# A hybrid decoder trunk on one core: the DeltaNet meta chunk as one padded block for two heads, key norms from a diagonal, loads issued ahead

## The chip, the core and the metric

The kernel runs on one core of one Trainium2 chip. The metric is the device time of one execution, in microseconds (us). The engines are TensorE (PE, with its weight loads as PEld), VectorE (DVE), ScalarE (ACT), GpSimd (POOL) and SyncE (SP, which here issues transfers). Each engine runs its own instructions in order; semaphores order them against each other.

## What is computed

Two layers over 528 tokens (16 learned meta tokens and 512 of the input) with 1024 channels: a forgetting attention with its feed-forward part, then a gated DeltaNet with its feed-forward part. The change touches the DeltaNet alone. Its core, per head of 128 channels (8 heads), with q and k normalised and chunks of up to 64 tokens in the reference:

```python
q = l2norm(q) * Dh ** -0.5;  k = l2norm(k)           # x * rsqrt(sum(x*x) + 1e-6)
dec = exp(where(i >= j, gc_i - gc_j, -inf))          # gc: running sum of the gates in a chunk
A = where(i > j, (k @ k.T) * dec * beta_i, 0)
W, U0 = triangular_solve(I + A, [k * beta * exp(gc), v * beta])
qk = (q @ k.T) * dec
# per chunk, in order:
U = U0 - W @ S.T
O = (q * exp(gc)) @ S.T + qk @ U
S = g_last * S + U.T @ (k * exp(gc_last - gc))
# then rmsnorm(O, o_gain) * silu(og) and the output projection
```

Everything is float32. The dense products split each float32 operand into a high and a low part, and sum three products.

## The kernel before

The tokens stand in two halves, 272 and 256 columns. A weight block of 128 output channels is a *unit*: `load` brings it in by SP, ACT makes its high part (L285), DVE or POOL its low part (L292), and `dense` (L312) runs 24 matmuls of 128x128 weights on 256 or 272 columns per half. L312 is most of TensorE's work everywhere.

The DeltaNet heads (`dn_heads`) run in four groups `g` of two heads (`NG = 2`, index `hl`). Here chunks are `CH`: one of the 16 meta tokens (`ci` 0) and four of 128 tokens. `DNSEQ` orders the units of K, V, Q, output gate (H) and the first half of the output projection (P). Each K, Q or V unit is followed by a causal convolution and a silu on ACT, DVE and POOL (`conv_tile`, L748 to L766, `proj`, L995 to L1004).

The rest of a group is a set of generators that a small planner, `Flow`, weaves in between the dense matmuls. Each `yield t` says when, in estimated TensorE time, the next step is issued; `flow.pe` advances that time, by 0.33 for three dense matmuls. The constants are `T_HOP`, `T_SUMS`, `T_BLOCKS`, `T_STEP`, `T_INV` and `T_OUT`. The steps are:

- `decays`: a transfer `gcr` of the gate sums, broadcast to all partitions, and exp(gc_i - gc_j) into `QD` (L1044, L1047).
- `gram_k`: squares of K on ACT (L1011), sums over the channels as matmuls with a column of ones (L1020), the norms' powers on POOL (L1063), then the products K with K (L1075), scaled into `AT` (L1082). `gram_q` does the same for Q against K (L1020, L1099, L1107), with one more transfer, `eg` (L1109), on the buffers of `gcr`.
- `solve_meta`: the inverse of the meta chunk's 16x16 block as a product of powers; all of its matmuls are 16x16, one per head (L1129, L1137).
- `solve`: the four 128-token chunks. Their 32x32 diagonal blocks go to DRAM (`dA`) and come back with one block on each partition (`AB`); POOL inverts them in 31 steps of two instructions (L1177, L1178); the result goes to DRAM (`dR`) and comes back as `Rc` (L1188). DVE transposes it into `Tc` (L1189), DVE and ACT copy it into the diagonal of `AT` (L1192), and four rounds of small matmuls (L1199 to L1235) finish the inverse.
- `scan`: chunk by chunk, transposes of V and K (L1256, L1257), K with the state S (L1260), `VB` (L1262, L1265), `U` (L1270, L1272), the new S (L1277, L1283) and the output product `po` (L1289, L1291). ACT copies it to `OU` and squares it (L1296, L1297).
- `heads_out`: the output norm's power on POOL (L1309), the scaling of `OU` on POOL (L1312), a transpose back on TensorE (L1316) and the gate.

A head's K, Q or V takes one of 16 buffers (`hd_tile`); when none is free, `flow.until` issues waiting steps, with no dense matmul between, until a scan has given its buffers back. A scan waits for the scan before it. PSUM has eight banks: two for dense results, two for `g` (sums and gram products), two for `s` (scan), one for `o` (`po`), one shared by `t` and `l`.

Dense matmuls and the scan's matmuls keep the order in which they were written (`tok`); the others, and all other engines, are placed by the build's scheduler.

## Time and profile before

| what | us |
|---|---|
| runs, median of 3 | 1601.74 (1598.82 to 1602.18) |
| the profiled execution | 1601.35 |
| its span, first to last instruction | 1599.4 |
| DeltaNet heads, as shown below | about 825 to 1174 of the span |
| TensorE, dense matmuls (L312) in the chain that ended last | 65% of the span |

Times in the profile count from the span's start. A row of a timeline has start, duration, engine, line, operation, out<-in, shapes and count, and in brackets the idle time ahead of it with what ended it. A matmul's duration contains its latency; what a matmul costs in a stream is the distance to the next one's start. A row that groups instructions has count, then busy time and mean ns of one, then the idle time ahead of them.

### The profile page before, as it was taken

To read this page: it belongs to the slowest core of one execution; us is meant where nothing else is said; L and a number is where in the kernel's file an instruction comes from. 1 tells how busy PE (TensorE), PEld (TensorE's weight loads), DVE (VectorE), ACT (ScalarE), POOL (GpSimd) and SP (SyncE) were. 2 spreads that over 40 slices of the span, in tenths; PEclk is the share of its full clock that TensorE was granted. 3 is DMA by queue.
4 is the path that set the end of the run, shared out by engine and by line. 5 is a ranking of instruction groups with operands and counts; after the bars stand their busy time and mean duration, and the time that the engine had idled before them with its cause. 6 is when DMAs were issued, how large, how long until landed. Compare 5 with 4: busy or idle time off the path is not lost.

```text
span 1599.4 us, 33295 instructions
## 1 busy us (share of the span) xinstructions
PE 1525.8 (95%) x12630; PEld 1486.8 (93%) x12630; DVE 1123.4 (70%) x2629; ACT 815.4 (51%) x1925; POOL 495.8 (31%) x993
## 2 busy tenths in 40 slices
PE   8999999999999999999789899899989999999996
PEld 6999999899999999999789798898989999999996
DVE  7888888948974675674978665676569864765764
ACT  6677777735643442343564456545456543432441
POOL 6434443025300010012556475654154200100112
PEclk9999999999999999999799998999999999999998
DMA  5232222422223222222323322222141323323321
GB/s 175 89 89 79 75 78 85 134 65 82 84 83 100 93 85 88 93 93 72 107 75 90 90 61 71 68 77 61 50 150 66 91 82 106 92 82 106 93 67 53
DMA packets 63327, 139.04 MB, mean 87 GB/s; under 512 B 18584, under 2 KB 31288, under 8 KB 62784
## 3 DMA queue, kind: packets, MB, share of 16 engines
q1 hardware_dynamic: 62544, 134.55, 28.1%
q8 instruction: 99, 1.62, 0.4%
q0 software_dynamic: 480, 2.15, 0.4%
q14 instruction: 60, 0.49, 0.1%
q10 hardware_dynamic: 144, 0.22, 0.0%
HBM read 131.54 MB, written 5.36 MB: 86 GB/s over the span
## 4 chain that ended last, share of the span: by engine, by line
PE 74%; DVE 11%; POOL 5%; DMA 4%; ACT 3%; issue 3%; SPq 1%; POOLq 0%; DVEq 0%; ACTq 0%
PE ps L312 65%; POOL PR L1177 2%; POOL RB L1178 2%; DVE h L412 1%; DVE bt L411 1%; DVE wl L292 1%; PE av L698 1%; DMA w<-wflat 1%; DVE cv L764 1%; DMA gcr<-gcd 1%; PE pt L678 1%; DVE xl L378 1%; ACT wh L285 1%; PE s L1277 1%; DVE qr L577 1%
## 5 line engine op out<-in xcount | busy, mean ns | idle before, releaser
L312 PE MATMUL ps<-xh,wh 128*128 128x256 f32 (+4 forms) x2464 | 717.6, 293 | 16.8 <-DVE ub L748 9.2
L312 PE MATMUL ps<-xl,wh 128*128 128x256 f32 (+4 forms) x2464 | 710.8, 289 | 3.4 <-DVE xl L378 3.0
L312 PE MATMUL ps<-xh,wl 128*128 128x256 f32 (+4 forms) x2464 | 713.6, 290 | 0.0
L312 PEld LDWEIGHTS ps<-xh,wh 128*128 128x128 f32 (+1 forms) x2464 | 469.6, 192 | 22.8 <-DVE ub L748 6.3
L312 PEld LDWEIGHTS ps<-xl,wh 128*128 128x128 f32 (+1 forms) x2464 | 471.1, 191 | 7.4 <-DVE xl L378 4.6
L312 PEld LDWEIGHTS ps<-xh,wl 128*128 128x128 f32 (+1 forms) x2464 | 471.1, 191 | 1.0
L285 ACT CAST wh<-w 128x1024 fp32r<-128x1024 f32 (+3 forms) x226 | 225.1, 997 | 189.5 <-PE ps L312 166.7
L292 DVE TENSOR_TENSOR wl<-w,wh 128x1024 fp32r<-128x1024 f32 (+4 forms) x191 | 220.6, 1156 | 99.3 <-ACT wh L285 98.7
L764 DVE SCALAR_TENSOR_TENSOR cv<-ub,prm,cv 128x256 f32<-128x256 f32 (+2 forms) x494 | 243.8, 498 | 38.4 <-ACT cv L755 29.5
L312 PE MATMUL ps<-ah,wl 128*128 128x256 f32 (+2 forms) x704 | 199.5, 284 | 0.0
L312 PE MATMUL ps<-ah,wh 128*128 128x256 f32 (+2 forms) x704 | 199.3, 283 | 0.0
L312 PE MATMUL ps<-al,wh 128*128 128x256 f32 (+2 forms) x704 | 199.1, 283 | 0.0
L755 ACT ACTIVATE cv<-ub,prm 128x256 f32<-128x256 f32 (+2 forms) x224 | 113.8, 511 | 146.3 <-DVE ub L748 146.2
L748 DVE TENSOR_TENSOR ub<-ps,r 128x256 f32<-128x256 f32 (+2 forms) x224 | 95.4, 428 | 101.5 <-PE ps L312 100.6
L353 POOL TENSOR_TENSOR ssq<-ssq,sq 128x256 f32<-128x256 f32 (+2 forms) x98 | 90.5, 926 | 144.5 <-ACT sq L352 143.0
L312 PEld LDWEIGHTS ps<-ah,wh 128*128 128x128 f32 x704 | 132.6, 189 | 0.0
L312 PEld LDWEIGHTS ps<-al,wh 128*128 128x128 f32 x704 | 132.5, 188 | 0.0
L312 PEld LDWEIGHTS ps<-ah,wl 128*128 128x128 f32 x704 | 132.4, 188 | 0.0
L751 POOL COPY cy<-ub 128x2 f32<-128x2 f32 (+1 forms) x112 | 38.0, 341 | 279.3 <-DVE ub L748 277.7
L292 POOL TENSOR_TENSOR wl<-w,wh 128x512 fp32r<-128x512 f32 x70 | 95.0, 1377 | 72.1 <-ACT wh L285 56.8
L747 POOL COPY ub<-cy 128x2 f32<-128x2 f32 (+1 forms) x112 | 31.3, 280 | 197.1 <-DVE cv L764 160.0
L786 ACT ACTIVATE gl<-cv 128x272 f32<-128x272 f32 (+2 forms) x88 | 36.7, 418 | 42.0 <-DVE cv L764 41.7
(308 smaller groups left out, 2454.5 us busy)
## 6 DMA issues: line engine op xcount, KB each, us to landing
w<-wflat SPq DMA_DIRECT2D x176, 512.0 KB, 3.5
w<-wflat SPq DMA_DIRECT2D x32, 448.0 KB, 3.3
cB<-cdram SPq DMA_DIRECT2D x16, 264.0 KB, 3.3
w<-wflat SPq DMA_DIRECT2D x16, 256.0 KB, 2.7
h<-h SPq DMA_DIRECT2D x8, 272.0 KB, 5.3
cB<-cdram SPq DMA_DIRECT2D x16, 136.0 KB, 3.0
h<-h SPq DMA_DIRECT2D x8, 256.0 KB, 5.0
AB<-dA SPq DMA_DIRECT2D x16, 128.0 KB, 3.2
```

What stands on the lines that cost most here:

```text
L285: nc.scalar.copy(wh[:], w32)
L292: eng.tensor_tensor(wl[:, c], w32[:, c], wh[:, c].bitcast(F32), op=ALU.subtract)
L312: tok(nc.tensor.matmul(o, w[:, a], r[:, c0:c1], start=(i == 0), stop=(i == tot - 1)))
L353: nc.gpsimd.tensor_tensor(self.acc[:, :n], self.acc[:, :n], sq[:, :n], op=ALU.add)
L747: nc.gpsimd.tensor_copy(ub[:, 0:c0], carry.pop(ft)[:, :c0])
L748: nc.vector.tensor_tensor(ub[:, c0:c0 + n], ps, r[:, :n], op=ALU.mult)
L751: nc.gpsimd.tensor_copy(c[:, :c0], ub[:, n:n + c0])
L755: nc.scalar.activation(cv, ub[:, c0:c0 + n], AF.Identity, scale=w[c0])
L764: nc.vector.scalar_tensor_tensor(cv, ub[:, i:i + n], w[i], cv, op0=ALU.mult, op1=ALU.add)
L786: nc.scalar.activation(g, cv, AF.Gelu_apprx_tanh)
L1177: nc.gpsimd.tensor_tensor(t, R3[:, 0:a, l:l + 1].to_broadcast([P, a, w]), A3[:, l:l + 1, l + 1:32].to_broadcast([P, a, w]), op=ALU.mult)
L1178: nc.gpsimd.tensor_tensor(R3[:, 0:a, l + 1:32], R3[:, 0:a, l + 1:32], t, op=ALU.subtract)
```

## The change

- **Meta chunk.** The two heads' 16x16 blocks stand at rows and columns 0 and 32 of one 128x128 tile that is otherwise zero. `solve_meta` then runs one full-size matmul for both heads (64 columns moving). The scan's first chunk is its own function, `scan_meta`, with full-size weights, one U product and one output product for both heads.
- **Key norms.** Squares and sums of K go. `gram_k` makes the key products first, and DVE multiplies each with the identity and sums along the rows (a reduce), which gives the norm from the diagonal. The factor 0.25 takes the place of the squares' scale 0.5.
- **Loads.** `decays` issues both `gcr` transfers and yields `T_DMA` before it reads them. `eg` is issued at the start of `gram_q`, on its own two buffers. A second transfer of `dR` writes the diagonal of `AT` in place of the copies (L1192), and the transpose into `Tc` is issued `T_BACK` later.
- **Output.** `po` is squared out of PSUM and scaled out of PSUM by ACT (head 0) and DVE (head 1); the ACT copy and POOL's scaling go. `po` has one bank, and is held until it is scaled.
- **Planner.** Constants change, and dense time is 0.0014 per column and group of three matmuls (0.38 for 272). `KD`, `VB`, `U` go from 3 buffers to 2, `S` from 5 to 4, `OU` from 2 to 1.

The diff, cut to its core:

```diff
-T_BLOCKS = 4
-T_STEP = 0.5
-T_INV = 10
+T_BLOCKS = 8
+T_DMA = 3.5
+T_STEP = 1.0
+T_META = 2.0
+T_BACK = 6
+T_INV = 3
...
-                flow.pe(0.33)
+                flow.pe(0.0014 * (c1 - c0))
...
+        def padded(name, i, w=P):
+            if (name, i) not in zeroed:
+                zeroed[name, i] = dp.tile([P, w], F32, name=f"{name}{i}")
+                nc.vector.memset(zeroed[name, i][:], 0.0)
+            return zeroed[name, i]
...
+                    gcrs.append(dp.tile([P, 272], F32, name="gcr", tag="gc", bufs=2))
+                    nc.sync.dma_start(gcrs[hl][:, :n], gcd[hd:hd + 1, s:s + n].to_broadcast([P, n]))
+                yield T_DMA
...
             def gram_k(half):
-                sqs = squares(half, K)
-                yield T_SUMS
-                pn = psum_tile("g")
-                sums(half, sqs, pn)
...
+                yield T_HOP
+                pgs = gram(half, K)
...
+                        dg = dp.tile([P, P], F32, name="dg", tag="osq")[:, 0:cn]
+                        nc.vector.tensor_tensor_reduce(out=dg, in0=pgs[hl][:, i * 128:i * 128 + cn], in1=ident[:, 0:cn], scale=1.0, scalar=0.0, op0=ALU.mult, op1=ALU.add, accum_out=y[:, c, hl:hl + 1])
+                nc.vector.tensor_scalar(y[:, cs, :], y[:, cs, :], 0.25, EPS, op0=ALU.mult, op1=ALU.add)
...
+            def gram(half, X):
...
+                        nc.tensor.matmul(pgs[hl][:, i * 128:i * 128 + cn], K[hl][:, c0:c0 + 128], X[hl][:, c0:c0 + cn], start=True, stop=True)
...
                 def products(*pairs):
                     ps = psum_tile("l")
-                        for hl in range(NG):
-                            nc.tensor.matmul(ps[:16, (i * NG + hl) * 16:(i * NG + hl) * 16 + 16], a[:, hl, :], b[:, hl, :], start=True, stop=True)
+                    for i, (x, y) in enumerate(pairs):
+                        nc.tensor.matmul(ps[:, i * 64:i * 64 + 64], x[:], y[:, b], start=True, stop=True)
...
+                    nc.sync.dma_start(AT[32 * b:32 * b + 32, :, 32 * b:32 * b + 32], dR[NC * b:NC * b + NC].rearrange("c j r i -> (j r) c i"))
+                yield T_BACK
                 nc.vector.transpose(Tc[:].rearrange("p c i -> p (c i)"), Rc[:].rearrange("p c i -> p (c i)"))
-                for b in range(4):
-                    bs = slice(32 * b, 32 * b + 32)
-                    (nc.scalar.copy if b % 2 else nc.vector.tensor_copy)(AT[bs, :, bs], Rc[bs])
...
+            def scan_meta(MO):
...
+                tok(nc.tensor.matmul(px[0][:, 128:256], st["Rm"][:], VB[:], start=True, stop=True))
...
+                for hl in range(NG):
+                    tok(nc.tensor.matmul(px[hl][:, 0:128], KD[hl][:], U[:], start=True, stop=True))
...
+                tok(nc.tensor.matmul(po[:, 0:128], st["QDm"][:], U[:], start=True, stop=True))
...
-                        nc.scalar.copy(OU[:cn, hl, :], oo)
-                        nc.scalar.activation(sq[:cn, 0:128], OU[:cn, hl, :], AF.Square, scale=128 ** -0.5, accum_out=MO[:cn, ci, hl:hl + 1])
+                        nc.scalar.activation(sq[:], po[:, hl * 128:hl * 128 + 128], AF.Square, scale=128 ** -0.5, accum_out=MO[:, ci, hl:hl + 1])
...
-                    nc.gpsimd.tensor_scalar(ot, ot, mo[:, hl:hl + 1], None, op0=ALU.mult)
+                    (nc.vector.tensor_scalar(OU[:, hl, :], po[:, hl * 128:hl * 128 + 128], mo[:, hl:hl + 1], None, op0=ALU.mult) if hl else
+                     nc.scalar.activation(OU[:, hl, :], po[:, hl * 128:hl * 128 + 128], AF.Copy, scale=mo[:, hl:hl + 1]))
...
-                yield lambda: ("gates", half) in done and (g < 2 or ("scan", g - 2) in done)
+                yield lambda: ("gates", half) in done and (g < 2 or ("scan", g - 2) in done) and (half or not g or ("meta", g - 1) in done)
```

Three places show how the instructions move. The rows give line, operation, out<-in and size; the changed kernel has its own line numbers (dense matmuls are L315, the scan's transposes L1295 and L1296, K with S L1298, U L1305, the new S L1311, the output products L1318 and L1319, the output transposes L1378).

First, TensorE in group 0's scan, just ahead of the next K unit; before, the last chunk's first products:

```order
L312 MATMUL ps<-xh_10425,wh 128x272
L312 MATMUL ps<-xl_10426,wh 128x272
L312 MATMUL ps<-xh_10425,wl 128x272
L1256 MATMUL s<-ident,hd 128x128
L1257 MATMUL s<-ident,hd 128x128
L1260 MATMUL s<-S,hd 128x128
L1256 MATMUL s<-ident,hd 128x128
L1257 MATMUL s<-ident,hd 128x128
L1260 MATMUL s<-S,hd 128x128
L312 MATMUL ps<-xh_10425,wh 128x272
```

The same place of the changed kernel, one chunk earlier:

```order
L1378 MATMUL t<-ident,OU 128x128 x2
L1305 MATMUL s<-VB,ATQD_11241 128x128 x2
L1311 MATMUL s<-U,KD 128x128 x2
L1318 MATMUL o<-S,hd 128x128
L1319 MATMUL o<-U,ATQD_11241 128x128
L1318 MATMUL o<-S,hd 128x128
L1319 MATMUL o<-U,ATQD_11241 128x128
L1295 MATMUL s<-ident,hd 128x128
L1296 MATMUL s<-ident,hd 128x128
L1298 MATMUL s<-S,hd 128x128
```

Before, dense matmuls stand between the steps of every chunk. Now the scan of group 0 is issued later, the buffers of K, Q and V run out first, and the work of its last three chunks stands in one piece of 36 rows with no dense matmul in it.

Second, DVE at the return of group 0's solve; before:

```order
L748 TENSOR_TENSOR ub<-ps,r 128x256
L764 SCALAR_TENSOR_TENSOR cv<-ub,prm,cv 128x272
L1192 COPY ATQD_11250<-Rc 32x8x32 x2
L1064 TENSOR_TENSOR rho<-y,rk 128x4
L764 SCALAR_TENSOR_TENSOR cv<-ub,prm,cv 128x272
L292 TENSOR_TENSOR wl<-w_12379,wh 128x1024
L1189 STREAM_TRANSPOSE Tc<-Rc 128x256
L1065 TENSOR_SCALAR rk<-rk 128x4
L1148 TENSOR_TENSOR Wm<-l,Wm 16x32
```

And in the changed kernel:

```order
L1178 TENSOR_TENSOR Y_11462<-l,ident 64x64
L1104 SCALAR_TENSOR_TENSOR ATQD_11736<-g,ab,ATQD_11736 128x128
L767 SCALAR_TENSOR_TENSOR cv<-ub,prm,cv 128x272
L751 TENSOR_TENSOR ub<-ps,r 128x256
L767 SCALAR_TENSOR_TENSOR cv<-ub,prm,cv 128x272
L295 TENSOR_TENSOR wl<-w_12584,wh 128x1024
L1132 TENSOR_SCALAR eq<-g 128x6
L1228 STREAM_TRANSPOSE Tc<-Rc 128x256
L1180 TENSOR_TENSOR Y_11460<-l,Y_11462 64x64
```

The copies are gone, and the first reader of `Rc` is the transpose, which now stands behind the key step of group 1 (L1104) that it stood ahead of before.

Third, ACT where a chunk's output is made, in a scan of group 0 before:

```order
L1296 COPY OU<-o 128x128 x2
L1138 COPY Wm<-l 16x32
L1262 ACTIVATE VB<-s,rho 128x128
L1297 ACTIVATE osq,MO<-OU 128x128
L1262 ACTIVATE VB<-s,rho 128x128
L1297 ACTIVATE osq,MO<-OU 128x128
L1266 ACTIVATE KD<-s,kd 128x128 x2
```

And in the scan of group 1 after:

```order
L1302 ACTIVATE KD<-s,kd 128x128
L1358 ACTIVATE osq,MO<-o 128x128
L1302 ACTIVATE KD<-s,kd 128x128
L1272 ACTIVATE ATQD_11736<-l 64x8x64
L1374 ACTIVATE OU<-o,MO 128x128
L1307 ACTIVATE U<-s,ub 128x128 x2
L1394 ACTIVATE o_12924<-t,osc 128x128
```

The square reads `po` itself, and the scaling (L1374), which reads POOL's power, stands ahead of the scan's next `U`.

More of the change, by code (lines that the diff above doesn't have):

```diff
@@ L1088, in gram_q @@
                 sqs = squares(half, Q)
+                egs = []
+                for hl in range(NG):
+                    hd = g * NG + hl
+                    egs.append(dp.tile([P, 272], F32, name="eg", tag="eg", bufs=2))
+                    nc.sync.dma_start(egs[hl][:, :n], gcd[hd:hd + 1, s:s + n].to_broadcast([P, n]))
                 yield T_SUMS
@@ new lines, in products @@
+                    return [ps[b, i * 64:i * 64 + 64] for i in range(len(pairs))]
+                nc.vector.tensor_tensor(N[b, b], N[b, b], smask[:], op=ALU.mult)
+                yield T_META
+                ps = psum_tile("l")
+                nc.tensor.transpose(ps[:, 0:P], N[:], ident[:])
+                nc.scalar.copy(NT[b, b], ps[b, b])
+                yield T_META
+                x, y = products((NT, N), (N, NT))
+                nc.scalar.copy(N2T[b, b], y)
+                nc.vector.tensor_copy(N2[b, b], x)
@@ new lines, in scan @@
+                    yield T_HOP + 0.6
+                    if ci < 4:
+                        for hl in range(NG):
+                            tok(nc.tensor.matmul(px[hl][:, 0:128], KD[hl][:], U[hl][:], start=True, stop=True))
+                            flow.pe(0.22)
+                            S[hl] = dp.tile([P, P], F32, name="S", tag="S", bufs=4)
+                            nc.vector.scalar_tensor_tensor(S[hl][:], S0[hl][:], GL[:, g * NG + hl, ci:ci + 1], px[hl][:, 0:128], op0=ALU.mult, op1=ALU.add)
```

219 lines of the change are left out of this document (116 added, 103 removed).

## The prediction

> **What bounds the kernel now.** First the page: busy shares, granted clock by slices, the chain that ended last.
>
> ```profile
> PE 1525.8 (95%) x12630; PEld 1486.8 (93%) x12630; DVE 1123.4 (70%) x2629; ACT 815.4 (51%) x1925; POOL 495.8 (31%) x993
> ...
> PEclk9999999999999999999799998999999999999998
> ...
> PE 74%; DVE 11%; POOL 5%; DMA 4%; ACT 3%; issue 3%; SPq 1%; POOLq 0%; DVEq 0%; ACTq 0%
> ```
>
> TensorE is busy for 95% of the span and holds 74% of the chain: what takes work from it shortens the run, and so does what ends a pause of it. The clock dips in the 20th and the 25th slice (40 us each); the latter, 960 to 1000 us, lies in the DeltaNet heads. Next the table of windows: the heads (825 to 1174 us) and four stretches in which the granted clock was half. Columns: start and end, length, busy time and count of PE, PEld, DVE, ACT, POOL, clock, DMA share, GB/s.
>
> ```profile
> 825.00:1174.00 349.00, 329.30 (x2952) 310.99 (x2950) 229.17 (x640) 181.93 (x529) 177.00 (x427) 0.95 0.28 75
> ...
> 900.70:907.50 6.80, 4.70 (x23) 4.37 (x23) 6.42 (x21) 3.09 (x6) 2.38 (x4) 0.50 0.31 84
> ...
> 975.80:986.00 10.20, 10.20 (x51) 8.31 (x51) 2.09 (x8) 2.69 (x10) 3.37 (x11) 0.50 0.39 100
> 1027.00:1030.40 3.40, 3.15 (x15) 3.07 (x16) 2.62 (x9) 3.04 (x10) 0.00 (x0) 0.50 0.22 45
> 1088.40:1091.90 3.50, 3.50 (x19) 3.50 (x19) 1.58 (x4) 1.82 (x3) 1.92 (x9) 0.51 0.00 0
> ```
>
> In the heads PE pauses for 349.00 - 329.30 = 19.7 us. Three of the half-clock stretches begin in or right behind a pause; the one at 975.8 follows none. The timelines name the pauses (in brackets the idle time before the row, and what ended it):
>
> ```profile
> 899.58 0.70 DVE L1192 COPY ATQD<-Rc 32x256 f32<-32x256 f32 x2 [7.98 <-DMA Rc<-dR]
> ...
> 902.80 0.28 PE L1129 MATMUL l<-Wm 16*16 16x16 f32 x4 [6.14 <-DVE Wm L1148]
> ...
> 957.67 0.41 ACT L1192 COPY ATQD<-Rc 32x256 f32<-32x256 f32 x1 [4.87 <-DMA Rc<-dR]
> ...
> 958.92 0.49 PE L1277 MATMUL s<-U,KD 128*128 128x128 f32 x2 [1.78 <-ACT U L1272]
> ...
> 1020.61 0.33 PE L1316 MATMUL t<-ident,OU 128*128 128x128 f32 x1 [1.96 <-POOL OU L1312]
> ...
> 1025.59 0.35 DVE L1044 SCALAR_TENSOR_TENSOR ATQD<-gcr,COL,dmask 128x128 f32<-128x128 f32 x1 [6.56 <-DMA gcr<-gcd]
> ...
> 1027.25 0.23 PE L1075 MATMUL g<-hd 128*16 128x16 f32 x2 [2.75 <-DVE ATQD L1107]
> ...
> 1088.16 0.33 PE L1316 MATMUL t<-ident,OU 128*128 128x128 f32 x1 [3.27 <-POOL OU L1312]
> ```
>
> In each an engine that runs its instructions in order stands at a late transfer, or POOL is late, with something for PE queued behind. At about 891.6 us DVE reached the Rc copy and waited 7.98 us for its transfer; L1148, for which PE waited, stood six rows behind (the order rows above).
>
> **What leaves PE.** The key sums (half of L1020). Their price is the group's row and one run of eight in PE's timeline:
>
> ```profile
> L1020 PE MATMUL g<-one,sq 128*128 128x1 f32 x160 | 20.0, 238 | 0.7 <-DVE ATm L1082 0.7
> ...
> 856.33 1.05 PE L1020 MATMUL g<-one,sq 128*128 128x1 f32 x8
> 857.24 0.37 PE L312 MATMUL ps<-xh,wh 128*128 128x272 f32 x1
> ```
>
> Eight rows take 857.24 - 856.33 = 0.91 us, 0.114 each. A float32 product is two rows, so the 40 of 80 sums that go are 80 rows: **9.1 us**.
>
> The small products of the meta chunk are priced as stops in the dense stream: from the dense row ahead to the second dense row behind, less two steady steps of 0.12.
>
> ```profile
> 860.70 0.28 PE L312 MATMUL ps<-xh,wh 128*128 128x256 f32 x1
> 860.91 0.26 PE L1129 MATMUL l<-Wm 16*16 16x16 f32 x4
> ...
> 861.33 0.28 PE L312 MATMUL ps<-xh,wl 128*128 128x256 f32 x1
> ...
> 875.01 0.29 PE L312 MATMUL ps<-xh,wl 128*128 128x272 f32 x1
> 875.14 0.38 PE L1099 MATMUL g<-hd 128*128 128x128 f32 x2
> ...
> 875.49 0.28 PE L312 MATMUL ps<-xl,wh 128*128 128x272 f32 x1
> ...
> 881.08 0.28 PE L312 MATMUL ps<-xh,wh 128*128 128x256 f32 x1
> 881.29 0.36 PE L1129 MATMUL l<-Wm 16*16 16x16 f32 x8
> ...
> 881.80 0.28 PE L312 MATMUL ps<-xh,wl 128*128 128x256 f32 x1
> ...
> 914.42 0.28 PE L312 MATMUL ps<-xh,wl 128*128 128x256 f32 x1
> 914.63 0.61 PE L1270 MATMUL s<-VB,Rm 16*16 16x128 f32 x4
> ...
> 915.39 0.28 PE L312 MATMUL ps<-xl,wh 128*128 128x256 f32 x1
> ...
> 918.35 0.28 PE L312 MATMUL ps<-xh,wl 128*128 128x260 f32 x1
> 918.55 0.71 PE L1277 MATMUL s<-U,KD 16*128 16x128 f32 x4
> ...
> 919.95 0.28 PE L312 MATMUL ps<-xl,wh 128*128 128x260 f32 x1
> ```
>
> A step of one product for two heads (four rows of 16x16) costs 0.63 - 0.24 = 0.39, a step of two products 0.72 - 0.24 = 0.48, and a full 128x128 product 0.48 - 0.25 = 0.23. A group has four steps of the first kind and two of the second: 2.52 before. Now a single block serves both heads: 4 x 0.23 + 2 x 0.46 = 1.84 at most, 0.7 less. In the scan the four Rm rows cost 0.97 - 0.24 = 0.73 and the KD and QDm rows 1.60 - 0.24 = 1.36; now there are four full products, 0.92, so 1.2 less. Over four groups: 4 x (0.7 + 1.2) = **7.6 us**. The meta key and query products (full weights for 16 columns) and one output transpose less I leave at nothing.
>
> Here the Trainium skill speaks against the padding: "TensorE: Matmul & The Clock Gate", section "LDWEIGHTS (loading the stationary operand)", has a weight load cost its columns over 1.2 ns, whatever the rows. By that a load of 16 columns is 13 ns and one of 128 is 107; an estimate from it, for the 54 small loads of a group that become 33 full ones, is 0.7 against 3.5 us, 11 us dearer over four groups, and a sum of 1604. The stops above hold their loads and come out the other way; a mechanism like the rule's is a rival below.
>
> **What ends waits.** The diff takes the Rc copies from DVE and ACT (a transfer writes AT, the transpose is issued 6 us later), the OU products from POOL, and starts gcr and eg transfers earlier on buffers of their own. So the pauses of 6.14, 1.78, 1.96, 2.75 and 3.27 us lose their causes: **15.9 us**. With three of them the half-clock stretches behind should go: PE was busy for 4.70 + 3.15 + 3.50 = 11.35 us there, half of which is **5.7 us**. In all 9.1 + 7.6 + 15.9 + 5.7 = **38.3 us**.
>
> **What is added.** (1) In the new order the last three chunks of the first scan stand on PE with no dense row between (above). Each round waits for an ACT and a DVE result, and its transposes (OT) for the output chain:
>
> ```profile
> L1272 ACT ACTIVATE U<-s,ub 128x128 f32<-128x128 f32 (+1 forms) x30 | 9.8, 360 | 5.4 <-PE s L1270 5.2
> L1265 DVE SCALAR_TENSOR_TENSOR VB<-s,COL,VB 128x128 f32<-128x128 f32 x24 | 8.0, 341 | 6.5 <-ACT VB L1262 6.4
> ...
> L1309 POOL TENSOR_TENSOR MO<-MO,mhalf x20: 692/721/1717, 924.4 to 1168.8; 128x2 f32<-128x2 f32 x16, 16x2 f32<-16x2 f32 x4
> ```
>
> At least 3 x (0.36 + 0.34) = 2.1 us. At most also two out-chain waits as long as the longest above, 3.27, and half clock throughout: 26 products at 0.23 = 6.0 us once more; 14.6. I take **9** (2.1, two waits of 1.96, half of the 6.0). (2) At the end two transposes stand right behind the last product that they depend on: 0 if the order is kept by slack, 3.27 at most; **3**. (3) The reduces, 40 on DVE, replace the key sums' squares on ACT:
>
> ```profile
> L650 DVE CUSTOM_DVE_ANT_0 S<-sc,cB 128x264 f32<-128x264 f32 x32 | 13.6, 427 | 0.3
> ...
> L650 DVE DVE_READ_ACCUMULATOR2_ANT st<- 128x1 f32 x96 | 7.9, 82 | 0.0
> ```
>
> No row has 128 columns; the nearest, 264, bounds them: 40 x (0.427 + 0.082) = 20 us of DVE. With DVE at 229 of 349 us the price on the path is 0 to 20; I take a quarter, **5**. (4) ACT and DVE now scale the output out of PSUM and wait for POOL's power (0.72 us, in POOL's queue among the steps of the solve), with conv and weight casts queued behind; PE waits for both. It happens in 20 rounds; a round can cost nothing, or the 1.96 of the nearest row: 0 to 39. I take what the old chain cost, 1.96 + 3.27 = **5.2**. (5) SP issues 16 more transfers of dR, with weight loads queued behind; one issue reads:
>
> ```profile
> 956.12 0.45 SPq L1188 DMA_DIRECT2D Rc<-dR  x1
> ```
>
> That is 16 x 0.45 = 7.2 us of SP in four places, hidden as long as the weights of the next units are loaded ahead; I take 0, and 7.2 if that cover is gone.
>
> Sum against the profiled execution, 1601.35 us (0.4 below the median, 1601.74): 1601.35 - 38.3 + 9 + 3 + 5 + 5.2 = 1585.3. I predict **1585**.
>
> **Rivals.**
> - *Waits only move.* PE's own 16.7 us go, but other waits of the length of the old ones come, and the crowded places cost 12: 1601.35 - 16.7 + 12 = 1596.7. For it: pauses come from one late transfer or another, and all of the order changes. Against: the causes named are taken away. 0.22.
> - *Nothing in the end.* As before, and the reduces also cost their 5: 1601.7, no change. For it: DVE carried 6.42 of the 6.80 us from 900.7. 0.09.
> - *The clock recovers.* The stretch at 975.8 goes too (half of 10.2, 5.1 us), and (1), (3), (4) come out at their low ends, 2.1 + 3: 1601.35 - 38.3 - 5.1 + 5.1 = 1563. 0.12.
> - *Slower: the output chain stalls ACT.* ACT's scale stands right ahead of the scan's next U rows (order above); if POOL's power is late by its queue each round, 20 rounds cost PE 1.96 each, 39 us: 1601.35 - 38.3 + 17 + 39 = 1619. It decides from (38.3 - 17) / 20 = 1.1 us a round. For it: L1309's longest took 1.72 us, and POOL is full during the solve. Against: ACT worked 182 of 349 us. 0.13.
> - *The padding costs.* A stop of four rows took 0.39 and one of eight 0.48: 0.30 fixed and 0.022 a small row, against 0.115 a full row. If the fixed part stays with full products among dense rows, a group pays 24 x 0.115 for 44 x 0.022, 1.8 us more, 7 over four: 1585.3 + 7.6 + 7 = 1600, no change. Against: the full product's stop above, 0.23 in all. 0.04. The skill's rule on weight loads points this way.
>
> The skill's clock rule is weighed too: "TensorE: Matmul & The Clock Gate", section "Part 1: The HAM clock gate (the \"warmup\" mystery)", has the clock halve after an idle window of about 3.4 us. The stretches behind the 6.14 and 3.27 us pauses agree; the one at 975.8, with PE busy throughout, does not. By the rule the crowded scan of (1) would keep full clock and the sum be 3 us lower.
>
> **How the numbers follow.** Forecast 0.40, the rivals 0.22, 0.09, 0.12, 0.13, 0.04. About 0.2%, 3.2 us, is what a measurement can tell from no change. Faster: 0.40 + 0.22 + 0.12 = 0.74; same 0.09 + 0.04 = 0.13; slower 0.13. The range holds forecast, moved waits, no change and padding (0.75) and the upper half of the clock case: 1566 to 1603, and (1) to (3) together at their low ends give 1570, (3) at its high end 1600.
>
> **What would show it.** Right: L1042 (sums) with 80 rows and some 10 us; no 6 us pause of PE behind a DVE wait on Rc; PE's pauses in the heads under 15 us. Wrong: PE waiting for OU from ACT or DVE in many rounds; ACT idle on POOL's power; a half-clock stretch over the first scan's end longer than 7 us; DVE busy above 290 us in the heads.

## The result, and the profile after

The changed kernel takes **1615.97 us** (median of 4 runs, 1615.81 to 1618.67), the kernel before 1600.75 on the same chip: ratio 1.0100, 95% interval 1.0082 to 1.0117. It is slower by 15 us; the prediction had it 16 us faster. The profiled execution has a span of 1614.3 us against 1599.4. The page of the changed kernel (busy time, granted clock in 40 us slices, the chain that ended last):

```profile
PE 1521.4 (94%) x12462; PEld 1489.7 (92%) x12462; DVE 1140.3 (71%) x2765; ACT 801.9 (50%) x1868; POOL 458.2 (28%) x951
...
PEclk9999999999999999999799789999998999999998
...
PE 68%; DVE 11%; POOL 6%; DMA 5%; ACT 4%; issue 3%; SPq 2%; POOLq 0%; DVEq 0%; ACTq 0%
```

PE's share of the chain fell from 74% to 68%: more of the chain is the work of other engines and of transfers. To see what PE lost, the heads are cut in both kernels at the same work: from the first column transpose to dense product 1632 of this phase. The tables of windows (start and end, length, busy time and count of PE, PEld, DVE, ACT, POOL, clock, DMA share, GB/s), before:

```profile
825.42:1181.88 356.46, 336.76 (x3014) 318.45 (x3013) 232.83 (x648) 185.56 (x537) 180.24 (x432) 0.95 0.29 78
```

and after:

```profile
828.40:1194.13 365.73, 328.99 (x2846) 318.83 (x2845) 247.11 (x769) 174.31 (x484) 145.76 (x388) 0.93 0.30 77
```

PE is busy 7.8 us less, and yet the stretch is 9.3 us longer. Its pauses rose from 356.46 - 336.76 = 19.7 to 36.7 us. The half-clock stretches inside, summed from the clock's records, rose from 34.1 to 51.2 us, with PE busy for 31.8 and 46.6 of them; half of that is lost. So **work at full clock fell by 15.2 us** (320.9 to 305.7), **pauses grew by 17.0** and **half clock cost 7.4 more**: +9.2. Another 3.0 us come ahead of the heads (they begin at 828.40, not 825.42) and 2.7 behind: 14.9 in all. What PE waited for in the heads (the table of waits: total us, times, longest), before:

```profile
PE l L1129 <- DVE Wm L1148: 6.1, 1, 6.1
PE t L1316 <- POOL OU L1312: 5.5, 3, 3.3
```

and after:

```profile
PE t L1378 <- ACT OU L1374: 9.9, 4, 4.5
PE ps L315 <- DVE ub L751: 8.8, 4, 3.5
PE s L1305 <- ACT KD L1302: 5.2, 4, 2.6
```

The longest pause of before (6.14, behind a DVE that stood at Rc) is gone; in its place stand many of up to 4.5 us, behind the output's scale, the conv's input and the scan's rows. The wait of the output transposes, behind which two of the pauses in the prediction lie, did not go: it rose from 5.5 us behind POOL to 9.9 behind ACT, which now does the scaling. One cause stands in the views of the tile Rc, which tell who waited for its transfer. Before:

```profile
  ACT ATQD L1192: 14.0, 3
  DVE ATQD L1192: 13.1, 3
```

After:

```profile
  ACT TM L1245: 15.4, 4
  DVE Tc L1228: 12.1, 4
```

27.1 us before, 27.5 after: the same standing, now at the transpose and at the copy behind it, with other rows queued behind that copy. The longest wait of the output transposes, 4.5 us, has this cause, on ACT:

```profile
1042.87 0.40 ACT L1245 COPY TM<-Tc 32x256 f32<-32x256 f32 x1 [6.58 <-DVE Tc L1228]
1043.30 0.37 ACT L1374 ACTIVATE OU<-o,MO 128x128 f32<-128x128 f32 x1
```

The other three (1.7, 1.5 and 2.2 us) come right behind a wait of ACT for POOL's power; the first of them, on ACT and on PE:

```profile
959.12 0.37 ACT L1374 ACTIVATE OU<-o,MO 128x128 f32<-128x128 f32 x1 [2.03 <-POOL MO L1371]
```

```profile
959.54 0.71 PE L1378 MATMUL t<-ident,OU 128*128 128x128 f32 x2 [1.72 <-ACT OU L1374]
```

Progress against dense products shows three places where much is lost. Windows of 24 dense products each (576 to 600, 1056 to 1080, 1536 to 1560), before:

```profile
955.97:968.11 12.14, 9.66 (x138) 8.23 (x137) 8.87 (x25) 9.01 (x26) 2.54 (x5) 1.00 0.27 65
1078.46:1082.72 4.26, 4.26 (x37) 4.09 (x35) 3.64 (x9) 3.19 (x10) 3.85 (x10) 1.00 0.28 65
1170.19:1173.29 3.10, 3.10 (x28) 3.10 (x27) 1.57 (x4) 1.02 (x4) 0.70 (x5) 1.00 0.62 259
```

After:

```profile
955.14:976.25 21.11, 15.23 (x92) 13.24 (x91) 13.29 (x39) 12.16 (x41) 3.55 (x11) 0.84 0.27 55
1076.28:1090.37 14.09, 11.04 (x83) 10.29 (x83) 5.91 (x18) 5.91 (x15) 11.15 (x35) 0.75 0.13 29
1176.50:1185.27 8.77, 6.51 (x43) 5.92 (x41) 3.51 (x10) 3.47 (x11) 1.43 (x5) 0.83 0.35 121
```

The first is the crowded scan of step (1), the third the tail of step (2), the second another piece of solve and scan rows without dense products that no step had. They are 9.0, 9.8 and 5.7 us longer, and the clock falls in each; the rest of the heads is some 15 us shorter. Not all of this is loss, since rows other than dense products also stand in other windows now: pauses make 3.4, 3.0 and 2.3 us of it and half clock 2.6, 2.7 and 1.4; the rest is work that stood elsewhere before.

### The profile page after: what moved, and what is told of

It is laid out like the page before. It is cut to its first block, busy times and chain, and to the rows that moved or that the text cites. A ratio compares the mean times of both kernels' runs of the same rounds, so it can differ in the third digit from the quotient of the medians.

```text
span 1614.3 us, 32996 instructions
## 1 busy us (share of the span) xinstructions
PE 1521.4 (94%) x12462; PEld 1489.7 (92%) x12462; DVE 1140.3 (71%) x2765; ACT 801.9 (50%) x1868; POOL 458.2 (28%) x951
## 4 chain that ended last, share of the span: by engine, by line
PE 68%; DVE 11%; POOL 6%; DMA 5%; ACT 4%; issue 3%; SPq 2%; POOLq 0%; DVEq 0%; ACTq 0%
PE ps L315 62%; POOL RB L1215 3%; POOL PR L1214 3%; DVE h L415 1%; DVE bt L414 1%; DVE wl L295 1%; DMA w<-wflat 1%; PE av L701 1%; DVE cv L767 1%; DVE xl L381 1%; DMA AB<-dA 1%; PE pt L681 1%; DMA gcr<-gcd 1%; ACT wh L288 1%; DVE qr L580 1%
## 5 line engine op out<-in xcount | busy, mean ns | idle before, releaser
L315 PE MATMUL ps<-xh,wh 128*128 128x256 f32 (+4 forms) x2464 | 720.6, 294 | 26.6 <-DVE ub L751 19.1
L315 PE MATMUL ps<-xl,wh 128*128 128x256 f32 (+4 forms) x2464 | 713.4, 290 | 6.1 <-DVE xl L381 6.0
L315 PE MATMUL ps<-xh,wl 128*128 128x256 f32 (+4 forms) x2464 | 716.3, 291 | 0.0
L315 PEld LDWEIGHTS ps<-xh,wh 128*128 128x128 f32 (+1 forms) x2464 | 473.9, 193 | 31.2 <-DVE ub L751 11.9
L315 PEld LDWEIGHTS ps<-xl,wh 128*128 128x128 f32 (+1 forms) x2464 | 474.3, 193 | 10.2 <-DVE xl L381 8.1
L315 PEld LDWEIGHTS ps<-xh,wl 128*128 128x128 f32 (+1 forms) x2464 | 474.1, 193 | 0.9 <-DVE wl L295 0.3
L315 PE MATMUL ps<-ah,wl 128*128 128x256 f32 (+2 forms) x704 | 199.8, 284 | 0.0
L315 PE MATMUL ps<-ah,wh 128*128 128x256 f32 (+2 forms) x704 | 199.6, 284 | 0.0
L315 PE MATMUL ps<-al,wh 128*128 128x256 f32 (+2 forms) x704 | 199.4, 284 | 0.0
L315 PEld LDWEIGHTS ps<-ah,wh 128*128 128x128 f32 x704 | 132.9, 189 | 0.0
L315 PEld LDWEIGHTS ps<-al,wh 128*128 128x128 f32 x704 | 132.7, 189 | 0.0
L315 PEld LDWEIGHTS ps<-ah,wl 128*128 128x128 f32 x704 | 132.6, 189 | 0.0
L814 DVE TENSOR_TENSOR m<-m,ps 128x256 f32<-128x256 f32 (+2 forms) x64 | 27.2, 425 | 42.6 <-PE ps L315 42.5
```

The source lines that it names most:

```text
L315: tok(nc.tensor.matmul(o, w[:, a], r[:, c0:c1], start=(i == 0), stop=(i == tot - 1)))
L814: nc.vector.tensor_tensor(mm, mm, ps, op=ALU.add)
```

## The experiments

In this table every row is one kernel: ratio to the kernel before on the same chip (with interval), and from its trace, cut as above, length of the heads, pauses of PE, half-clock time and PE's work at full clock, in us. The trace is one execution, and executions of one kernel differ: the kernel before took 1596.0 to 1609.3 us in the 29 runs beside p_norm. The last column is rough as well, because it takes half of the busy time at half clock as lost: j_up (316.4) and n_both (318.2) have all rows that PE has before (320.9). Differences of under 5 us in it say little where the half-clock time differs.

| kernel | ratio | length | pauses | half clock | work |
|---|---|---|---|---|---|
| before | 1 | 356.5 | 19.7 | 34.1 | 320.9 |
| changed | 1.0100 (1.0082-1.0117) | 365.7 | 36.7 | 51.2 | 305.7 |
| p_norm | 1.0032 (1.0017-1.0048) | 360.7 | 30.0 | 51.2 | 309.9 |
| p_pad | 1.0017 (1.0002-1.0031) | 353.4 | 26.8 | 37.6 | 311.2 |
| p_out | 1.0010 (0.9995-1.0025) | 357.3 | 19.2 | 37.6 | 322.5 |
| p_plan | 1.0051 (1.0031-1.0071) | 362.1 | 24.7 | 34.1 | 321.2 |
| p_load | 1.0022 (1.0006-1.0037) | 359.4 | 19.7 | 37.6 | 321.3 |
| j_up | 1.0039 (1.0022-1.0056) | 364.9 | 20.4 | 61.4 | 316.4 |
| n_none | 0.9985 (0.9973-0.9997) | 352.2 | 25.9 | 30.7 | 313.7 |
| n_both | 0.9999 (0.9988-1.0010) | 358.7 | 14.1 | 54.6 | 318.2 |
| n_half | 0.9985 (0.9972-0.9998) | 354.3 | 18.7 | 34.1 | 319.7 |
| a_plan0 | 1.0130 (1.0110-1.0150) | 376.7 | 44.6 | 61.4 | 304.6 |
| a_load0 | 1.0073 (1.0055-1.0091) | 364.5 | 36.5 | 54.6 | 302.8 |
| a_back | 1.0127 (1.0106-1.0149) | 373.0 | 42.5 | 51.2 | 307.3 |
| a_jit | 1.0080 (1.0061-1.0098) | 364.6 | 38.3 | 41.0 | 307.0 |
| a_norm0 | 1.0041 (1.0028-1.0053) | 363.9 | 30.3 | 37.6 | 316.5 |
| a_free | 1.0080 (1.0063-1.0097) | 365.3 | 36.8 | 51.2 | 305.2 |
| p_free | 0.9990 (0.9977-1.0004) | 354.1 | 25.3 | 34.1 | 312.6 |
| b_two | 1.0040 (1.0026-1.0055) | 361.6 | 39.7 | 41.0 | 304.1 |
| b_three | 1.0052 (1.0034-1.0070) | 362.5 | 37.7 | 47.8 | 304.6 |

**One part at a time, on the kernel before.** Diagonal norms alone:

```diff
-                sqs = squares(half, K)
-                sums(half, sqs, pn)
...
+                        nc.tensor.matmul(pgs[hl][:, i * 128:i * 128 + cn], K[hl][:, c0:c0 + 128], K[hl][:, c0:c0 + cn], start=True, stop=True)
...
+                        nc.vector.tensor_tensor_reduce(out=dg, in0=pgs[hl][:, i * 128:i * 128 + cn], in1=ident[:, 0:cn], scale=1.0, scalar=0.0, op0=ALU.mult, op1=ALU.add, accum_out=y[:, c, hl:hl + 1])
```

> The kernel before with one part of the change: key norms from the diagonal of the key products (40 reduces on DVE, no key sums on PE, no key squares on ACT), the key products with 128 weight columns for the meta chunk too. All else as before (1600.75 us). Theory A (the 15 us come from scan and solve rows that the planner's constants and the loads push into one piece): the sums' 9.1 us leave PE and nothing crowds: 1590 to 1597. Theory B (the output path costs): the same. Theory C (DVE carries the heads, so the reduces give the gain back): 1599 to 1606, with PE waits behind DVE in the heads up by 5 us or more. Theory D (any change of the order moves waits by several us whatever it is): 1592 to 1612 without a pattern.

1.0032, and 1607 us, just above the range of theory C and inside that of theory D; the 9.1 us do not come. PE's work falls by 11.0 us, pauses grow by 10.3, half clock by 17.1. Much of that is one half-clock stretch of 27.3 us, from 907.24 to 934.54. The padded meta chunk alone (solve_meta and scan_meta of the change):

> The kernel before with one part of the change: the meta chunk of two heads as one zero-padded block in solve and scan, with the steps' due times and smaller buffer counts that came with it. Output path, loads, norms and the other planner constants as before. My prediction put this part at -7.6 us. Theory A: 1592 to 1599. Padding rival (the fixed part of a product stays): 1602 to 1610, and the 33 full products of a group take more of PE than the 54 small ones. Theory D: anything from 1590 to 1612, the difference then being in pauses of PE and not in PE's busy time.

1.0017. The time lies in the range of the padding rival, but its mechanism does not: work falls by 9.7, and the heads are 3.1 us shorter. That is given back ahead of the heads (they begin at 828.45) and behind. The output path alone:

```diff
-                    nc.gpsimd.tensor_scalar(ot, ot, mo[:, hl:hl + 1], None, op0=ALU.mult)
+                    nc.scalar.activation(OU[:cn, hl, :], po[:cn, hl * 128:hl * 128 + 128], AF.Copy, scale=mo[:, hl:hl + 1])
```

(DVE takes the second head.)

> The kernel before with one part of the change: ACT squares the output straight from PSUM and ACT and DVE scale it out of PSUM behind POOL's power; POOL's scaling and ACT's copy are gone. All else as before. Theory B (this chain stalls ACT and with it the scan): 1607 to 1620, with ACT idle on POOL's MO in many rounds and PE's U wait longer than the 5.2 us that it has before. Theory A: 1596 to 1602, the pauses of 1.96 and 3.27 us behind POOL's OU shorter. Theory D: 1590 to 1612.

1.0010, no difference to be told from none; 1604 us lies between theory A and theory B. ACT does stand 11.9 us for POOL's power over 20 rounds, 0.6 a round, and PE's pauses do not grow:

```profile
L1311 ACT ACTIVATE OU<-o,MO 128x128 f32<-128x128 f32 (+1 forms) x20 | 7.2, 359 | 12.0 <-POOL MO L1307 11.9
```

The planner's constants alone:

```diff
-T_BLOCKS = 4
-T_STEP = 0.5
+T_BLOCKS = 8
+T_STEP = 1.0
-                flow.pe(0.33)
+                flow.pe(0.0014 * (c1 - c0))
```

> The kernel before with the planner's constants of the change alone: blocks 8 in place of 4, steps 1.0 in place of 0.5, a dense product booked by its columns. No instruction is added or removed, only moved. Theory A in its plainest form: 1606 to 1615, with the first scan's last chunks in one piece without dense rows and 24 dense rows there taking 20 us in place of 12. Theory B and the padding rival: 1599 to 1603. If it is the loads and not the constants that delay the scan, this one is same, and the loads alone are slower.

1.0051, the dearest part alone, and in the range of theory A. Its first crowded place takes 19.8 us, as expected, and its last 24 dense products 8.57 us in place of 3.10, as in the changed kernel. PE's timeline there:

```profile
1169.96 0.38 PE L1291 MATMUL o<-U,ATQD 128*128 128x128 f32 x2
1173.37 1.06 PE L1316 MATMUL t<-ident,OU 128*128 128x128 f32 x2 [3.03 <-POOL OU L1312]
```

and the window of those 24 products:

```profile
1167.82:1176.39 8.57, 5.43 (x34) 4.95 (x33) 2.51 (x6) 2.87 (x10) 2.65 (x7) 0.78 0.35 122
```

The output transposes stand right behind the last product they depend on: a pause of 3 us, then half clock on the dense products. So the constants alone are enough to make the tail's loss. The loads alone (transfers ahead, AT from a second transfer, transpose 6 us later, T_INV 3 in place of 10):

> The kernel before with the loads of the change alone: gcr and eg transfers issued ahead on their own buffers, the solve's result read into AT by a second transfer, the transpose of Rc planned 6 us after its transfer. My steps put most of the 15.9 us of pauses here. If those pauses go and stay gone: 1585 to 1594. Theory E (they come back elsewhere, as in the changed kernel, where DVE and ACT together stand 27.5 us for Rc, against 27.1 before): 1600 to 1612.

1.0022, as theory E had it: nothing of the 15.9 us comes. The 6.14 us pause is gone and the output transposes wait 2.8 us in place of 5.5, yet PE's pauses are 19.7 us in all, as before. Other waits fill the place, the largest of them short or absent before:

```profile
PE s L1280 <- ACT KD L1276: 6.5, 4, 3.8
PE g L1022 <- ACT sq L1013: 2.5, 1, 2.5
```

**What an order, or a load, costs by itself.** One number moved by 3%:

```diff
-                flow.pe(0.33)
+                flow.pe(0.34)
```

> The kernel before with one number of the planner moved a little: a dense product booked at 0.34 us in place of 0.33. The same instructions, in another order from the heads' solve on. It measures how far an order alone moves the time. Theory D (any other order moves waits by several us): off by 3 to 10 us from 1601, either way. If it stays within 2 us, the +2 to +8 us of the single parts are theirs and not the order's.

1.0039: the same instructions in another order cost 6 us, more than any single part but the constants. A single part's time therefore proves little; only what its trace shows at a place does, or several kernels together. The key norms left out:

> The kernel before with the key norms left out: no key squares, no key sums, a constant in their place; nothing added. PE has 80 rows, about 9 us, less to do and ACT 40 squares less. If the heads are bound by PE's work, 1591 to 1594, and then the reduces of the change are what gave the gain back. Theory E: 1598 to 1604, PE's pauses in the heads up from 19.7 to 25 us or more with nothing added to DVE.

0.9985, as theory E had it: 7.2 us less work, 6.2 us more pauses, 2 us gained. And the reduces added, read by nobody:

> The kernel before with the 40 reduces on DVE added and read by nobody; key squares and sums stay. This is the price of the reduces alone. If DVE's load is what counts (my term of 5, at most 20): 1606 to 1620. If DVE has room there: 1600 to 1604, and the loss with the diagonal norms comes from their place in the chain (power and scales wait for the products), not from DVE's time.

0.9999: 40 reduces on DVE cost nothing that can be told from an order's effect.

**The changed kernel in other orders.** With the constants of before:

> The changed kernel with the planner's constants of before (blocks 4, steps 0.5, a dense product booked at 0.33 us); padding, norms, output path and loads stay changed. The changed kernel takes 1615.97 us; the constants alone cost the kernel before some 8 us (0.5%). Theory A (the constants push scan and solve into places without dense products): 1604 to 1609, the 21 us place at dense product 576 to 600 and the 14 us place at 1056 to 1080 gone or under 2 us longer than before. Theory E (PE's saved work turns into pauses in whatever order, since results of other engines and transfers are awaited): 1610 to 1617, pauses in the heads still over 30 us.

1.0130, above both ranges. The crowded places nearly go, as theory A asked: dense products 576 to 600 take 14.3 us in place of 21.1 (12.1 before), with 0.7 us of pauses and 6.8 us at half clock, and 1056 to 1080 take 3.9. The tail's pause of 2.3 us stays, without half clock. The first place and the tail:

```profile
972.21:986.54 14.33, 13.66 (x144) 13.14 (x143) 6.29 (x19) 7.39 (x24) 1.30 (x4) 0.76 0.11 38
1190.68:1196.83 6.15, 3.84 (x30) 3.46 (x29) 2.00 (x6) 2.67 (x9) 1.43 (x5) 1.00 0.38 127
```

Yet the kernel gains nothing: PE's pauses in the heads are 44.6 us, more than the 36.7 of the changed kernel, and lie elsewhere. With the loads of before (T_INV too):

> The changed kernel with the loads of before: Rc copied to AT by DVE and ACT, transposed at once, gcr and eg read where they were. If the loads are what costs the 15 us: 1598 to 1604. Theory E: 1610 to 1624, like the other orders of the changed kernel (1616 and 1626).

1.0073, in the range of theory E: the loads are not what costs most, and their share is no larger than what an order makes. With T_BACK 12 in place of 6:

> The changed kernel with the transpose of Rc planned 12 us after its transfer in place of 6. In the changed kernel DVE stands 12.1 us for Rc and ACT 15.4 us behind it, in four solves. If the planned distance is what was too short: those waits under 8 us together and 1606 to 1612. If it only delays the solve and what waits for it: 1614 to 1625.

1.0127, as was expected if it only delays: the waits for Rc fell only to 8.4 (DVE) and 13.1 (ACT). With a dense product booked 3% longer:

> The changed kernel with a dense product booked 3% longer (0.00144 us a column in place of 0.0014): the same instructions in another order. With before, j_up (1608) and the changed kernel's other order (1626) it shows whether the orders of the changed kernel lie above those of before. If the change itself costs: 1610 to 1626. If 1616 was a bad draw among orders: 1596 to 1608.

1.0080. Four orders of the changed kernel lie at 1.0080 to 1.0130, above every order of the kernel before that was run (1, 1.0039, 1.0051). That speaks for a cost of the change itself, and against 1616 as a bad draw among orders.

**The norms and their tiles.** The key step of group 0 in the changed kernel (key products on PE, power and first solve step on POOL):

```profile
836.72 0.85 PE L1114 MATMUL g<-hd 128*128 128x16 f32 x6
...
858.52 1.06 PE L1114 MATMUL g<-hd 128*128 128x128 f32 x8
```

```profile
850.99 2.63 POOL L1093 TENSOR_TENSOR rk<-y,mhalf 128x6 f32<-128x6 f32 x1 [3.46 <-DVE y L1092]
...
875.73 0.47 POOL L1214 TENSOR_TENSOR PR<-RB,AB 128x31 f32<-128x31 f32 x1 [1.11 <-DMA AB<-dA]
```

and in the kernel before:

```profile
838.07 1.51 POOL L1063 TENSOR_TENSOR rk<-y,mhalf 128x6 f32<-128x6 f32 x1 [3.44 <-DVE y L1062]
840.37 1.01 POOL L1063 TENSOR_TENSOR rk<-y,mhalf 128x4 f32<-128x4 f32 x1
...
857.96 0.24 POOL L1177 TENSOR_TENSOR PR<-RB,AB 128x31 f32<-128x31 f32 x1 [4.97 <-DMA AB<-dA]
```

Before, the power comes ahead of the products, and both halves' powers stand side by side. Now the products are written first and hold both PSUM tiles of kind "g" until the power is back and the scaling has read them; the second half's products follow 21.8 us behind the first (before, 4.5), and the solve begins at 875.73, not 857.96. To test that, the norms of before in the changed kernel:

> The changed kernel with the key norms of before (squares on ACT, 80 rows of sums on PE, the power before the key products). Theory F (the key products come first and hold both PSUM tiles of kind g through reduces, power and scales, so the second half's key products wait for the first half's last key row, and the solve starts late: group 0's first solve step at 876 us, 858 before): the first solve step back at 858 to 864, both halves' powers within 5 us of each other, and 1603 to 1610 although PE gets 80 rows more. If the norms are not the cause: first solve step still after 870, or 1612 to 1624.

1.0041, 0.6% better than the changed kernel with 80 PE rows more; the time lies just above what was expected. The place is not as expected: first solve step at 870.0, powers 10.8 us apart. The other test frees the tiles in p_norm: the multiplication with the decays moves right behind the reduces, and ACT scales later.

```diff
+                        nc.vector.tensor_tensor(a, o, d, op=ALU.mult)
...
-                        nc.vector.scalar_tensor_tensor(a, o, ab[:cn, c, hl:hl + 1], d, op0=ALU.mult, op1=ALU.mult)
+                        nc.scalar.activation(a, a, AF.Copy, scale=ab[:cn, c, hl:hl + 1])
```

> The diagonal norms alone (as p_norm, 1607), but DVE multiplies the key products with the decays right behind the reduces, which frees the PSUM tiles before the power, and ACT scales the result afterwards (40 more ACT instructions a run). Theory F: the second half's key products no longer wait for the power of the first; in p_norm they started 16 us behind the first half's (848.4 and 832.1), now under 10; the first solve step at or before 862 (866.4 in p_norm); 1598 to 1604. If only the length of the chain counts and not the held tiles: 866 and 1605 to 1610.

0.9990 against 1.0032, and 1601 us as expected; the difference, 0.4%, is as large as what an order makes. PE's timeline of p_norm, the second half's products 16.4 us behind the first:

```profile
832.06 0.85 PE L1061 MATMUL g<-hd 128*128 128x16 f32 x6
...
848.43 0.61 PE L1061 MATMUL g<-hd 128*128 128x128 f32 x4
```

and of p_free, 8 us behind:

```profile
832.79 0.85 PE L1061 MATMUL g<-hd 128*128 128x16 f32 x6
...
840.76 0.69 PE L1061 MATMUL g<-hd 128*128 128x128 f32 x4
```

That the held tiles delay the products is shown at this place, that they cost the time is not; the first solve step, 863.3, came 1.3 us later than expected. In the changed kernel the same edit:

> The changed kernel with the same edit. Theory F: the first solve step at 862 to 870 in place of 876, and 1606 to 1613. If the held tiles do not matter: 1613 to 1624.

1.0080, and 1617 us, in the range named for held tiles that do not matter. The second half's products come 10.9 us behind the first in place of 21.8, but the first solve step, at 878.5, does not come earlier.

**Does saved work count at all?** Diagonal norms with freed tiles and padding together, all else as before:

> The parts that pay or nearly pay, on the kernel before: diagonal norms with the PSUM tiles freed before the power (p_free, ratio 0.999) and the padded meta chunk (p_pad, 1.0017); constants, loads and output path of before. PE's work in the heads falls by some 18 us against before. If PE's work counts once the chain is not delayed: 1588 to 1596. If, as with the key sums left out (0.9985), saved PE work turns into pauses: 1598 to 1606.

1.0040, and 1609 us, above both ranges: 16.8 us less work, 20.0 us more pauses. The largest share is the output transposes' wait for POOL's scaling, 12.7 us where it was 5.5, though this kernel has the output path of before.

```profile
828.98:1190.61 361.63, 321.92 (x2847) 313.05 (x2845) 242.74 (x762) 190.49 (x549) 170.88 (x423) 0.94 0.28 76
```

With the output path as well:

> The same with the output path of the change as well (p_out by itself 1.001). Expected as b_two, within the 6 us that an order alone can make: 1590 to 1608; clearly slower than b_two would say that the scaling out of PSUM costs in this company.

1.0052, not to be told from b_two, and 1611 us, above the range as well. And the solve shortened (every second step left out):

```diff
-                for l in range(31):
+                for l in range(0, 31, 2):
```

> The kernel before with every second step of the solve on POOL left out (16 steps of 31, a different result), nothing else. PE's work is unchanged; POOL has some 70 us less to do, and each group's solve is up to 17 us shorter. If the chain of a group (key step, solve, transfer, scan) sets the length of the heads: 1580 to 1592, PE's pauses in the heads well under 19.7 us. If only the order of the rows counts: 1596 to 1608, like the other orders of the kernel before.

0.9985, inside the second range: the run gains 2 us. The four transposes of Rc come 12.6, 21.3, 16.4 and 8.1 us earlier, but what PE does with them (L1214) starts 0.1, 2.7, 22.5 and 9.1 us earlier: in the first two groups the shorter solve did not reach PE. In the last two it did, and the heads got no more than 2.2 us shorter. So nothing points to the solve's length as what sets the end. None of the 18 kernels beats the kernel before by more than 0.15%, and the two at 0.9985 leave work out.

## Why the prediction was wrong, step by step

**What leaves PE** was right. The terms of 9.1 and 7.6 us measured 11.0 (p_norm) and 9.7 (p_pad) alone, 15.2 together in the changed kernel against 16.7, in a column that is good to some 5 us. The rows of the sums, the reduces and the output's scale after:

```profile
L1042 PE MATMUL g<-one,sq 128*128 128x1 f32 x80 | 11.1, 259 | 2.2 <-DVE ATQD L1104 2.2
L1091 DVE CUSTOM_DVE_ANT_0 dg<-g,ident 128x128 f32<-128x128 f32 (+1 forms) x40 | 10.1, 254 | 0.3
...
L1374 ACT ACTIVATE OU<-o,MO 128x128 f32<-128x128 f32 x20 | 7.4, 368 | 16.2 <-POOL MO L1371 15.5 <-PE t L1378 0.6
```

The rule on weight loads (the Trainium skill, "TensorE: Matmul & The Clock Gate", section "LDWEIGHTS (loading the stationary operand)"), from which the prediction estimated padding to be 11 us dearer, does not fit these traces: p_pad's work fell, and loads of 16 columns (L1129 before) took 89 ns each where it gives 13, loads of 128 (L1160 after) about 200 where it gives 107.

**What ends waits is the step that failed.** It took 15.9 us of pauses as gone because their causes are taken away, and 5.7 us of half clock with them; with the 22.2 us that it added, the prediction had waits and clock at 0.6 us in all. They came out at 24.4: the pauses in the heads went from 19.7 to 36.7 us, and half clock cost 7.4 more. (The rest of the 14.9 us is 15.2 less of work, and 5.7 more outside the heads, which no step had and which one trace of each kernel does not explain.) Two of the five named pauses went, those of 6.14 and 2.75 us; the waits of the other three stand there still. PE waits for ACT's U for 1.9 us (1.8 before) and for the output's scale for 9.9 (5.5 before), and the engines stand as long for Rc as before. What the step had wrong is that it treated a pause as the property of one wait. p_load shows it with all of PE's rows kept: there the longest pause went, and others of the same sum came. In the table, work and pauses go against each other: kernels with 316 to 323 us of work pause 14 to 25 us (a_norm0 30), those with 310 to 314 pause 25 to 30, those with 303 to 307 pause 37 to 45. Within what the column can tell, work taken from PE came back as pauses almost one for one, also where nothing was added (n_none) and where the tiles were freed early (b_two).

**What is added.** (1) The crowded first scan was right, also in kind: 9 us taken, of which 6.0 waits and 3.0 half clock; its window has 5.9 us of pauses and 2.6 lost to half clock, at a clock of 0.84. That its length grew by 9.0 is chance: 2.9 of that is work that stood elsewhere, and the window before had 2.5 us of pauses too. A second such place, 5.8 us of pauses and half clock, was overlooked. Yet with the pauses of both places gone (a_plan0) the kernel is no faster. (2) The tail was right in kind and somewhat too small: 3 taken, 2.3 of pause and 1.4 of half clock behind it measured; the constants alone make it (p_plan), but its pause stays without them (a_plan0). (3) The reduces take 13.2 us of DVE (10.1 and 3.1 for reading the sums out), inside the bounds, but the 5 us on the path cannot be seen (n_both, 0.9999). So what the diagonal norms cost is not DVE's time. They put the power behind the products, which hold their PSUM tiles; p_norm against p_free (0.4%) and a_norm0 against the changed kernel (0.6%) speak for that, a_free (0.2%) does not, and an order alone is worth 0.4%. (4) The scale's wait for POOL's power was taken at 5.2; p_out alone is 1.6 us, not to be told from 0. ACT stands 15.5 us in 20 rounds, 0.78 a round. (5) The transfers on SP: the loads as a whole cost 0.2%, which an order could make.

**The rivals.** "Waits only move" named the right mechanism with too small a price (1596.7): waits moved, and grew by as much as the work fell. "Slower: the output chain stalls ACT" gave 1619, near the result, mostly by luck. Its mechanism is there, but small: 0.78 us a round lies below its deciding 1.1, PE waited behind POOL's power and ACT's scale in three rounds, 5.4 us, and p_out costs nothing that can be measured. Of the signs named for a right prediction the 80 rows of sums and the missing 6 us pause came, and pauses under 15 us did not. Of those named for a wrong one ACT's standing for POOL's power came; PE waited for ACT's OU in 4 rounds, not in many, DVE was busy 247 us, not 290, and the half-clock stretch over the first scan lasted 6.8 us (960.5 to 967.3).

**What stays open.** Why pauses take the place of PE's work. DVE's load (n_both), the solve's length (n_half, in two groups of four), the loads, the output path and the constants were each tried and none sets the end alone. The parts alone add up to 1.3% and all together cost 1.0%; since one number of the planner is worth 0.4%, part of this may be that the order of before fits its instructions better than any order tried since. That is argued, not shown. A planner fed with measured durations was not tried.

## What to carry to other kernels

In a stretch where PE is 95% busy but runs between chains of other engines, a microsecond taken from PE is not a microsecond won: leave the work out altogether first (as n_none) and see what that alone brings. Where a scheduler decides the order, run the kernel with one neutral number moved before reading anything into half a per cent. And when a value is taken from a product instead of being computed ahead of it, ask what the product's buffer waits for: here it began to be held through a round trip over three engines.

## What the runs showed of the clock

The half-clock stretches of all 20 traces begin on one grid of 3.41 us within a run, and they do not need an idle PE. The kernel before, two windows of this grid and the stretch behind:

```profile
968.97:972.38 3.41, 3.41 (x32) 3.34 (x31) 1.81 (x6) 2.56 (x13) 1.07 (x3) 1.00 0.53 104
972.38:975.80 3.42, 3.42 (x33) 2.75 (x33) 1.63 (x3) 2.18 (x7) 1.13 (x3) 1.00 0.27 62
975.80:986.00 10.20, 10.20 (x51) 8.31 (x51) 2.09 (x8) 2.69 (x10) 3.37 (x11) 0.50 0.39 100
```

PE is busy without a gap in the second window, and half clock follows for 10.2 us. What sets it apart from a window of dense products is the width of its rows: among the 33 are sums of one column and 16 products of 64, in all 2361 columns, where a window of dense products moves some 7500. Over the 20 traces (826 to 1186 us, each row's columns counted in the window in which it ends), 1830 windows at full clock give: under 1000 columns, half clock follows in 47 of 47; 1000 to 2000 in 45 of 54; 2000 to 3000 in 42 of 92; 3000 to 4000 in 11 of 125; from 4000 on in 0 of 1512. Eighteen of those that were followed by half clock had PE busy for over 90%. Behind narrow rows the clock was also slow to come back. In p_norm it stayed low for eight windows, in which PE was busy for 20.08 of 27.30 us:

```profile
907.24:934.54 27.30, 20.08 (x180) 18.61 (x180) 14.91 (x47) 9.42 (x23) 13.48 (x42) 0.50 0.21 50
```

This fits the stretch at 975.8 that the prediction left without a cause, though with 2361 columns it could as well have kept its clock (42 of 92). It also fits that pieces of scan and solve without dense products lose the clock: their rows are narrow. No run changed the width of the rows alone, so that the width is the cause is not shown. The Trainium skill ("TensorE: Matmul & The Clock Gate", section "Part 1: The HAM clock gate (the \"warmup\" mystery)") has the window of 3.4 us right; that an idle window is needed does not agree with these runs, nor did the crowded scan keep full clock (0.84), as the prediction worked out by that rule.
